# Hybrid RG-LRU and RWKV-7 block: two plain input-projection tiles go from the first stage to the preparation of the second recurrence

## The chip, the cores and the metric

The kernel runs on one core of a Trainium2 chip. The metric is device time in microseconds (us) of one execution. The engines are PE (TensorE matmul), PEld (TensorE weight load, which overlaps PE), DVE (VectorE), ACT (ScalarE), POOL (GpSimd) and SP (SyncE, which issues nearly all DMAs here).

## The reference, cut to what matters

One layer with 1024 latent tokens and 256 context tokens, model width 1024. The modulated input `h` is projected once by `w_in`; the columns of the product are split between the RG-LRU branch (`ux`, `uy`), the RWKV-7 branch (`r`, `k`, `v` and small low-rank inputs) and the two merge gates (`gl`, `gr`):

```python
ux_l, uy_l, zr_l, gl_l, gr_l = jnp.split(h_lat @ p['w_in'], pts, axis=-1)
hf_l, _ = lru_dir(ux_l, sf, p, 0, False)          # first recurrence, both directions
hb_l, _ = lru_dir(ux_l, sb, p, 1, True)
lru_l = ((hf_l + hb_l) * jax.nn.gelu(uy_l)).astype(h_lat.dtype)
rw_l, _ = rwkv_branch(centred_shift(to_colmajor(zr_l, rows), p['rwkv_mu']), S_c, p, True)
out_l = merge(lru_l, rw_l, gl_l, gr_l, p)         # sigmoid(gl), sigmoid(gr) as gates
```

After it follow the output projection, a SwiGLU channel mixer and a final norm. `uy`, `gl` and `gr` are used only after the second recurrence has begun, so their projection can be done at any time before that.

## The kernel before, in words

All projections run as float32 split in two parts: `mm3` (L87 to L90) issues three matmuls of 128x512 per 128x128 weight block, and so every output tile of 128 channels costs 8 blocks x 3 matmuls per 512 tokens. `inproj` (L218) computes one tile `m` of `w_in`: it loads the weights in two halves (`wraw`, 256 KB each), DVE casts each half to the high part (`whi`, L230), POOL subtracts for the low part (`wlo`, L231), and PE runs the matmuls into PSUM tiles named `pin{m}_{column}`. The tiles by number: 0 to 9 are `ux`, 10 to 19 `uy`, 20 to 27 `r`, 28 to 35 `k`, 36 to 43 `v`, 44 to 46 the low-rank inputs, 47 to 54 `gl`, 55 to 62 `gr`. (The small projection `w_gd2` in `gate` carries number 47 too.)

A *plain* tile is one of the 26 tiles of `uy`, `gl` and `gr`. `plain` (L289) is a generator that computes them one by one: 2 x 24 matmuls over the latent tokens, then ACT copies each PSUM half to `ev` (L296) and SP stores it to DRAM (L297). Nothing in the two stages below reads them.

**First stage**, `phase_ux` (L243): the ten `ux` tiles, then `NFILL - NEND` plain tiles with the eight `v` tiles spread evenly among them (for-loops at L266 to L277), then `NEND` = 3 plain tiles. The first recurrence (`lru_tiles`, 36 units of DVE, ACT, POOL and PE work) runs through all of this as a generator that is advanced at given points: after plain tile number q it has come to step 24 x (4 + 2 x min(1, (q+1)/10)). A `v` tile is projected over all 1280 tokens, shifted on DVE and ACT (`zv`, L493, L499), transposed on PE and stored.

**Preparation of the second recurrence**, `phase_a2` (L813): first the low-rank inputs (tiles 44 to 46, the first two over 1280 tokens) and the output gate, then ten units (0 and 1 for the context, 2 to 9 for one head pair each). A unit projects `k` and `r`, and in four sub-steps builds the operands of the second recurrence (`pz`, `kb`, `kr`, `kt`, `pm`, `km`). After units 1, 3, 5, 7, 8 and 9 their 32x32 triangular matrices are inverted on DVE (`wkv_inverse`, L724 and L725, 31 steps), in pieces between the sub-steps of the next units. The plain tiles that `phase_ux` left over are filled in by `due(x)`: after sub-step x of 40, x/38 of the `26 - NFILL` tiles must have been issued.

The second recurrence and everything behind it (`phase_b`, `phase_c1`, `phase_c2`) follow. The order of instructions on each engine is laid out when the program is built, by a scheduler that takes priorities from the code; on the chip each engine works through its own list in that order.

Of the kernel before, what the change touches and what calls it, by code (L numbers as in the profile page):

```python
# [242 lines left out]
def phase_ux(k):  # L243
    nc = k.nc
    k.inbufs = 3
    with k.tc.tile_pool(name="pux", bufs=1) as pool, k.tc.tile_pool(name="psux", bufs=2, space=PSUM) as ps, \
# [17 lines left out]
        fill = plain(k)  # L264
        n = NFILL - NEND
        for q in range(n):  # L266
# [13 lines left out]
            next(fill)  # L280


NFILL = 15
VEV = 2
INLO = 1
POFF = 400
# [526 lines left out]
def phase_a2(k, hc):  # L813
# [3 lines left out]
    with tc.tile_pool(name="pprep", bufs=1) as k.prep, tc.tile_pool(name="pzr", bufs=1) as k.zrp, tc.tile_pool(name="pa2c", bufs=1) as cp, \  # L817
# [50 lines left out]

        fill = plain(k, NFILL)
        nd = FILLA  # L870
# [3 lines left out]
        def due(x):  # L874
            for (a, b), (c, d) in zip(FPTS, FPTS[1:]):
                if x <= c:
                    return (b + (d - b) * (x - a) / (c - a)) * (26 - NFILL)
            return 26 - NFILL

# [806 lines left out]
```

## Time and profile before

| what | us |
|---|---|
| median of the runs (3 runs, 3083.84 to 3108.86) | 3095.47 |
| the profiled execution | 3079.55 |
| its span, first to last instruction | 3077.7 |
| PE busy, PEld busy | 2707.6 (88%), 2159.6 (70%) |
| DVE busy, ACT busy, POOL busy | 1890.6, 1456.4, 1012.4 (61%, 47%, 33%) |

The span falls into four parts: `ux` up to about 285 us, `v`, plain tiles and first recurrence up to about 715, the preparation of the second recurrence up to about 1520, and the rest. The changed lines lie in the second and third. A row of the windows view gives the busy time of each engine in a stretch, the count of instructions, the granted TensorE clock (1.00 is 2.4 GHz, 0.50 is 1.2 GHz) and the DMA share. Busy shares are averages; what a stretch is bounded by is read from the waits in it.

### The profile page before, as it was taken

Reading aid. Unit: us, or ns where it says so; the run is one execution under the profiler, and the core shown is the slowest. Engines: PE = TensorE matmul, PEld = TensorE weight load, DVE = VectorE, ACT = ScalarE, POOL = GpSimd, SP = SyncE. Lnnn points to the kernel's source line nnn. Section 1 sums busy time; section 2 is a strip of 40 time slices with the busy share of each in tenths; the row PEclk is TensorE's granted clock in tenths of the full one; section 3 lists DMA queues with packets and bytes.
Section 4 is the critical chain, followed back from the end, with each engine's and each line's share of the span. In section 5 each row is a group of like instructions: output and inputs, shape, how many; then the busy total and the mean of one; then the engine's idle time right before and its main releaser. Section 6 shows DMA issues by size and latency. Waiting matters only on the chain. (4 is left out here: it accounts for less than half of the span.)

```text
span 3077.7 us, 57133 instructions
## 1 busy us (share of the span) xinstructions
PE 2707.6 (88%) x22526; PEld 2159.6 (70%) x22526; DVE 1890.6 (61%) x2843; ACT 1456.4 (47%) x2647; POOL 1012.4 (33%) x896
## 2 busy tenths in 40 slices
PE   5988988889899878887889788777999999999998
PEld 4776766667677666676656666555788888888888
DVE  7588898994667977889872333564785323223234
ACT  3476777783467565767433343454334111111114
POOL 4344444452445555666333130235431000000000
PEclk9899999999999979988569998888999999999999
DMA  5333334322455456556766787988753111121112
GB/s 207 95 117 123 124 104 134 111 85 77 133 152 146 119 123 141 124 137 158 200 196 218 228 258 220 253 252 261 269 214 127 58 48 50 41 61 42 42 57 73
DMA packets 379602, 429.18 MB, mean 139 GB/s; under 512 B 134166, under 2 KB 286150, under 8 KB 371398
## 3 DMA queue, kind: packets, MB, share of 16 engines
q1 hardware_dynamic: 379334, 425.53, 47.4%
q8 instruction: 178, 2.92, 0.4%
q14 instruction: 90, 0.74, 0.1%
HBM read 286.87 MB, written 126.26 MB: 134 GB/s over the span
## 5 line engine op out<-in xcount | busy, mean ns | idle before, releaser
L88 PE MATMUL pin<-h1024hi,whi 128*128 128x512 f32 (+1 forms) x1024 | 430.5, 421 | 47.5 <-DVE whi L230 15.4
L90 PE MATMUL pin<-h1024hi,wlo 128*128 128x512 f32 (+1 forms) x1024 | 420.9, 414 | 10.7 <-POOL wlo L231 10.6
L89 PE MATMUL pin<-h1024lo,whi 128*128 128x512 f32 (+1 forms) x1024 | 425.8, 416 | 4.1 <-DVE h1024lo L120 4.1
L231 POOL TENSOR_TENSOR wlo<-wraw,whi 128x512 fp32r<-128x512 f32 (+1 forms) x144 | 211.7, 1471 | 306.6 <-DVE whi L230 167.8
L88 PEld LDWEIGHTS pin<-h1024hi,whi 128*128 128x128 f32 (+1 forms) x1024 | 203.3, 199 | 102.0 <-DVE whi L230 15.9
L90 PEld LDWEIGHTS pin<-h1024hi,wlo 128*128 128x128 f32 (+1 forms) x1024 | 201.5, 197 | 64.5 <-POOL wlo L231 17.7
L89 PEld LDWEIGHTS pin<-h1024lo,whi 128*128 128x128 f32 (+1 forms) x1024 | 203.4, 199 | 50.0 <-DVE h1024lo L120 6.6
L54 ACT ACT_TABLE_LOAD x164 | 210.4, 1283 | 18.3 <-DVE gd L499 5.9
L987 PE MATMUL pn<-tvu,ska 128*64 128x64 f32 (+1 forms) x2496 | 157.4, 250 | 36.1 <-ACT tvu L990 19.2
L1434 DVE TENSOR_TENSOR sil<-sil,pfu 128x512 f32<-128x512 f32 x44 | 30.3, 688 | 242.0 <-PE pfu L90 242.0
L388 DVE SCALAR_TENSOR_TENSOR lxc<-lup,c_lru_conv_w,lxc 120x512 f32<-120x512 f32 (+3 forms) x198 | 161.1, 837 | 15.9 <-ACT lxc L386 15.2
L987 PEld LDWEIGHTS pn<-tvu,ska 128*64 128x64 f32 (+1 forms) x2496 | 119.9, 156 | 71.8 <-ACT tvu L990 23.8
L1442 DVE SCALAR_TENSOR_TENSOR x<-pfo,modv,x 128x512 f32<-128x512 f32 (+1 forms) x112 | 74.2, 671 | 132.4 <-PE pfo L90 132.4
L990 ACT COPY tvu<-ru 32x256 f32<-32x256 f32 x193 | 70.1, 363 | 126.8 <-DVE tvu L990 77.8
L68 ACT CAST whi_fi<-wraw_fi 128x1024 fp32r<-128x1024 f32 x48 | 50.5, 1053 | 167.6 <-PE pfg L89 50.4
L724 DVE TENSOR_TENSOR it<-bp,X 128x62 f32<-128x62 f32 (+25 forms) x186 | 122.1, 657 | 3.9
L230 DVE CAST whi<-wraw 128x512 fp32r<-128x512 f32 (+1 forms) x144 | 76.3, 531 | 76.3 <-PE pin L89 36.6
L687 ACT COPY bc<-pm 32x256 f32<-32x256 f32 x160 | 98.8, 617 | 50.9 <-PE pm L683 48.4
L673 PE MATMUL pkt<-c_ident,kb 128*128 128x128 f32 x320 | 59.2, 315 | 65.6 <-DVE kb L657 41.5
L987 PE MATMUL ru<-tvu,skb 128*32 128x64 f32 (+1 forms) x2560 | 93.0, 243 | 26.8 <-ACT tvu L990 8.7
L725 DVE TENSOR_TENSOR X<-X,it 128x62 f32<-128x62 f32 (+25 forms) x186 | 113.7, 611 | 3.9
L432 POOL TENSOR_TENSOR lxc<-la 120x512 f32<-120x512 f32 (+3 forms) x66 | 86.8, 1318 | 80.1 <-ACT la L54 68.3
(374 smaller groups left out, 7512.9 us busy)
## 6 DMA issues: line engine op xcount, KB each, us to landing
skb<-skb_d SPq DMA_DIRECT2D x40, 1024.0 KB
wraw<-in_w_in_dram SPq DMA_DIRECT2D x142, 256.0 KB
wraw_fi<-in_w_ffn_in_dram SPq DMA_DIRECT2D x48, 512.0 KB
skb_d<-kr SPq DMA_DIRECT2D x160, 128.0 KB
ska_d<-kt SPq DMA_DIRECT2D x160, 128.0 KB
skb_d<-km SPq DMA_DIRECT2D x160, 128.0 KB
ska<-ska_d SPq DMA_DIRECT2D x40, 512.0 KB
wmr<-in_w_modT_dram SPq DMA_DIRECT2D x32, 512.0 KB
```

Source lines behind the costliest of these rows:

```text
L54: ins = self.nc.scalar.activation(*a, **b).ins
L88: nc.tensor.matmul(out, wh, xh, start=first, stop=False)
L89: nc.tensor.matmul(out, wh, xl, start=False, stop=False)
L90: nc.tensor.matmul(out, wl, xh, start=False, stop=last)
L230: nc.vector.tensor_copy(hi, raw)
L231: (nc.gpsimd if INLO else nc.vector).tensor_tensor(lo, raw, hi.bitcast(F32), ALU.subtract)
L388: nc.vector.scalar_tensor_tensor(xc, tap(j), k.lcw[r, t, d, j:j + 1], xc, ALU.mult, ALU.add)
L432: nc.gpsimd.tensor_tensor(xc, a, a, ALU.mult)
L687: nc.scalar.copy(bc[g, :, 4 * i:4 * i + 4].rearrange("s t e h -> s h e t"), pm[64 * c + 32:64 * c + 64, :, d, :, 32:64])
L724: nc.vector.tensor_tensor(tv, bpt[:, :, t + 1:32, t:t + 1].to_broadcast(sh), X[:, :, t:t + 1, 0:t + 1].to_broadcast(sh), ALU.mult)
L725: nc.vector.tensor_tensor(X[:, :, t + 1:32, 0:t + 1], X[:, :, t + 1:32, 0:t + 1], tv, ALU.add)
L987: k.pe_last = nc.tensor.matmul(*a, **b, start=True, stop=True).ins.name
```

## The change

```diff
-NFILL = 15
+NFILL = 13
```

`NFILL` stands in two places. In `phase_ux` the loop that carries the eight `v` tiles now runs over 10 plain tiles and not 12; the three at the end stay. In `phase_a2`, `plain(k, NFILL)` begins two tiles earlier in the list and `due` spreads 13 tiles and not 11 over the same 40 sub-steps. Every tile keeps its own work: the counts of instructions on PE, DVE, POOL and SP are the same, and ACT has 162 table loads for 164.

**End of the first stage, ACT.** Here the copies out of PSUM show in which order the tiles end: `ev49`, `ev50`, `ev51` are plain tiles, `vt7` is the last `v` tile, `held16` the first low-rank tile (`pin44`) of the next stage, `lg010_1_1` and `la10_1_1` belong to the last unit of the first recurrence. Before:

```order
L296 COPY ev49_0_5981<-pin49_0_5919 128x512
L572 COPY vt7_0_5892<-pv7_0_5893 128x512
L296 COPY ev49_512_5984<-pin49_512_5920 128x512
L572 COPY vt7_512_5900<-pv7_512_5901 128x512
L296 COPY ev50_0_6049<-pin50_0_5987 128x512
L572 COPY vt7_1024_5908<-pv7_1024_5909 128x256
L296 COPY ev50_512_6052<-pin50_512_5988 128x512
L296 COPY ev51_0_6117<-pin51_0_6055 128x512
L296 COPY ev51_512_6120<-pin51_512_6056 128x512
L509 COPY held16_6261<-pin44_0_6171 128x512
```

All of these stand behind the last step of the first recurrence. Now:

```order
L54 ACTIVATE lg110_1_1_5642<-pg10_1_1_5633,c_lru_bx_510 80x512
L296 COPY ev49_0_5981<-pin49_0_5919 128x512
L54 ACT_TABLE_LOAD
L54 ACTIVATE lg010_1_2_5425<-lg010_1_2_5425 80x512
L54 ACT_TABLE_LOAD
L54 ACTIVATE la10_1_1_5649<-lg010_1_1_5640,cneg_543 80x512
L54 ACTIVATE lg010_1_1_5640<-lg010_1_1_5640,cpos_540 80x512
L296 COPY ev49_512_5984<-pin49_512_5920 128x512
L54 ACT_TABLE_LOAD
L54 ACTIVATE lg010_1_1_5640<-lg010_1_1_5640 80x512
L509 COPY held16_6125<-pin44_0_6035 128x512
```

The last plain tile of the stage (49) now ends inside the last unit of the recurrence; tiles 50 and 51 are gone from here, the last `v` tile has moved ahead of the recurrence's end, and the first low-rank tile follows at once.

**The same place, DVE.** The operations of the last unit of the recurrence (`lg010_1_1`, `la10_1_1`, `lho10`) and the weight casts (`whi45` is the second low-rank tile). Now:

```order
L434 SCALAR_TENSOR_TENSOR lg010_1_1_5640<-lxc10_1_1_5409,lg010_1_1_5640 80x512
L445 TENSOR_TENSOR lg010_1_1_5640<-lg010_1_1_5640,lg110_1_1_5642 80x512
L447 SCALAR_TENSOR_TENSOR la10_1_1_5649<-la10_1_1_5649,la10_1_2_5432,lg010_1_1_5640 80x512
L455 TENSOR_TENSOR lho10_5647<-la10_0_1_4950,la10_1_1_5649 80x8x64
L230 CAST whi45_0_6154<-wraw45_0_6152 128x512
```

Before, five weight casts of the tiles 50, 51 and 44 stood between `lho10` and `whi45`; now `whi45` follows on `lho10` directly.

**Preparation, end of the third inverse, DVE.** `X4` is the matrix being inverted, `xo4` its result, `whi60` and `whi61` the weights of plain tiles, `zr8` the next `r` tile. Before:

```order
L734 STREAM_TRANSPOSE xo4_13265<-X4_11705 64x32x32
L658 SCALAR_TENSOR_TENSOR av5_256_1_12596<-kk7_12010,av5_256_1_12596 128x256
L657 TENSOR_TENSOR kb5_0_1_12633<-kd15_0_1_12630,ep5_0_1_12625 128x8x32
L689 TENSOR_TENSOR km4_768_1_12466<-pm4_768_12425,msk_6169 128x512
L230 CAST whi61_0_13282<-wraw61_0_13280 128x512
L230 CAST whi61_1_13312<-wraw61_1_13310 128x512
L499 SCALAR_TENSOR_TENSOR zr8_12771<-pin26_0_12772,c_mu_545,zr8_12771 128x512
```

Now:

```order
L725 TENSOR_TENSOR X4_11705<-X4_11705,it4_30_13262 128x2x31
L733 STREAM_TRANSPOSE xo4_13265<-X4_11705 64x32x32
L734 STREAM_TRANSPOSE xo4_13265<-X4_11705 64x32x32
L733 STREAM_TRANSPOSE xo4_13265<-X4_11705 64x32x32
L734 STREAM_TRANSPOSE xo4_13265<-X4_11705 64x32x32
L230 CAST whi60_1_12968<-wraw60_1_12966 128x512
L499 SCALAR_TENSOR_TENSOR zr8_12703<-pin26_0_12704,c_mu_545,zr8_12703 128x512
```

A whole plain tile (61) stood behind the third inverse; now half of tile 60 stands behind it and the other half inside it. Of the halves of plain tiles, 18 of 22 stood ahead of the third inverse's end before, and 21 of 26 stand there now. Counted over all projection tiles (plain, `k` and `r`), the inverse after unit 1 and the stretch behind it hold as many as before; the inverse after unit 3 holds half a tile more, the stretch behind it half a tile more, the inverse after unit 5 half a tile more, the stretch behind it as many, and the inverse after unit 7 half a tile more. That makes the two tiles.

## Rows read from the trace of the kernel before

**Rows 1.** Windows: busy us per engine (instructions), granted clock, DMA share; first stage.
```profile
285.00:690.00 405.00, 349.48 (x1540) 268.70 (x1539) 362.54 (x496) 307.94 (x460) 188.86 (x159) 0.95 0.36 111
690.00:710.00 20.00, 14.25 (x60) 11.24 (x59) 10.23 (x14) 16.56 (x22) 6.91 (x5) 0.83 0.12 34
710.00:790.00 80.00, 78.90 (x370) 60.51 (x369) 40.05 (x70) 19.93 (x30) 20.02 (x21) 1.00 0.26 80
```
**Rows 2.** Waits of DVE and of PE, 285 to 690: total us, times, longest.
```profile
DVE lg L445 <- ACT lg L54: 23.4, 6, 6.0
DVE lg L434 <- POOL lxc L432: 7.1, 8, 1.6
...
PE pg L415 <- DVE ll L399: 11.0, 9, 3.2
```
**Rows 3.** Timeline of PE: start us, us, engine, line; spacing of projection matmuls.
```profile
714.87 0.40 PE L88 MATMUL pin<-h1024hi,whi 128*128 128x512 f32 x1
...
717.20 0.40 PE L89 MATMUL pin<-h1024lo,whi 128*128 128x512 f32 x1
...
698.48 0.63 PE L89 MATMUL pin<-h1024lo,whi 128*128 128x512 f32 x1
...
701.47 0.63 PE L90 MATMUL pin<-h1024hi,wlo 128*128 128x512 f32 x1
...
317.99 0.28 PE L88 MATMUL pin<-h256hi,whi 128*128 128x256 f32 x1
...
318.70 0.28 PE L88 MATMUL pin<-h256hi,whi 128*128 128x256 f32 x1
```
**Rows 4.** Timeline: last gate matmul, last recurrence step, start of the second low-rank tile.
```profile
686.68 0.39 PE L415 MATMUL pg<-lh,gw 80*80 80x512 f32 x1
...
712.06 1.04 DVE L455 TENSOR_TENSOR lho<-la,la 80x512 f32<-80x512 f32 x1
...
751.28 0.40 PE L88 MATMUL pin<-h1024hi,whi 128*128 128x512 f32 x1
```
**Rows 5.** Operations on the tile zv (a v tile), DVE: duration ns min/median/max.
```profile
L499 DVE SCALAR_TENSOR_TENSOR zv<-held,c_mu,zv x32: 723/742/1796, 340.2 to 709.5; 128x512 f32<-128x512 f32 x16, 128x511 f32<-128x511 f32 x16
...
L499 DVE SCALAR_TENSOR_TENSOR zv<-pin,c_mu,zv x16: 452/472/486, 342.6 to 710.2; 128x255 f32<-128x255 f32 x16
```
**Rows 6.** Windows: preparation of the second recurrence, inverses and stretches between them.
```profile
790.00:979.00 189.00, 175.61 (x1401) 145.46 (x1399) 118.46 (x186) 126.65 (x272) 100.35 (x114) 0.95 0.61 159
979.00:1061.00 82.00, 67.15 (x523) 51.74 (x524) 79.72 (x120) 45.71 (x89) 46.28 (x47) 0.88 0.49 119
1061.00:1116.00 55.00, 36.54 (x371) 29.91 (x371) 35.66 (x56) 41.68 (x85) 33.17 (x41) 0.74 0.61 134
1116.00:1190.00 74.00, 59.41 (x423) 46.79 (x422) 72.56 (x107) 33.88 (x66) 35.00 (x35) 0.87 0.46 108
1190.00:1272.00 82.00, 77.21 (x659) 62.79 (x660) 53.70 (x83) 55.83 (x111) 55.62 (x63) 0.96 0.59 140
1272.00:1350.00 78.00, 62.84 (x515) 50.63 (x513) 76.09 (x114) 46.83 (x91) 44.20 (x46) 0.89 0.51 123
1350.00:1407.00 57.00, 55.38 (x504) 45.52 (x505) 43.80 (x65) 42.82 (x86) 39.35 (x45) 0.94 0.64 158
1407.00:1486.00 79.00, 47.77 (x554) 39.17 (x552) 77.25 (x116) 54.95 (x101) 51.58 (x58) 0.70 0.74 189
```
**Rows 7.** Weight casts (L230) and weight subtractions (L231), 790 to 1486: ns min/median/max.
```profile
L230 DVE CAST whi<-wraw x68: 363/428/1554, 791.3 to 1410.3; 128x512 fp32r<-128x512 f32 x68
...
L231 POOL TENSOR_TENSOR wlo<-wraw,whi x69: 1263/1307/1742, 788.8 to 1410.8; 128x512 fp32r<-128x512 f32 x69
```
**Rows 8.** Timeline of DVE and POOL: inverse steps beside a weight subtraction.
```profile
995.31 0.61 DVE L725 TENSOR_TENSOR X<-X,it 128x440 f32<-128x440 f32 x1
...
998.37 1.71 DVE L724 TENSOR_TENSOR it<-bp,X 128x462 f32<-128x462 f32 x1
...
998.13 1.45 POOL L231 TENSOR_TENSOR wlo<-wraw,whi 128x512 fp32r<-128x512 f32 x1
```
**Rows 9.** Windows: end of the preparation and start of the second recurrence.
```profile
1440.00:1450.00 10.00, 3.95 (x44) 3.55 (x44) 9.75 (x19) 5.89 (x6) 7.45 (x8) 0.50 0.78 193
...
1500.00:1540.00 40.00, 38.39 (x397) 26.96 (x397) 33.08 (x83) 11.95 (x23) 9.35 (x13) 0.50 0.62 154
1540.00:1580.00 40.00, 34.46 (x357) 23.10 (x357) 31.56 (x50) 16.72 (x29) 13.13 (x11) 0.51 0.69 193
```

## The prediction

> **What bounds the kernel now.** The page gives shares over the whole span, and these hide that the two stages the change touches have different limits. So I read the windows view first, stage by stage, and in each stretch looked for the engine that is never free.
>
> In the stretch with `v`, plain tiles and the first recurrence, 285 to 690 us, no engine is full: DVE is busy 362.5 of 405 us (90%), PE 349.5 (86%), ACT 307.9 [rows 1]. What DVE waits for there is the recurrence itself: ACT for `lg` 23.4 us, POOL for `lxc` 7.1 us, and PE in turn waits for DVE to make `ll` [rows 2]. So the stretch is paced by a chain that goes round DVE, ACT and POOL, and PE's projection tiles lie in its holes, not always neatly. From 710 to 790 the picture turns: PE is busy 78.9 of 80 us at full clock, DVE half [rows 1]. There the recurrence is over, and PE works off what is left of the stage: plain tiles, then the low-rank tiles that open the next stage.
>
> The preparation alternates. While an inverse runs (979 to 1061, 1116 to 1190, 1272 to 1350, 1407 to 1486), DVE is busy 97 to 98% and PE 60 to 82%; between them PE is the fuller one (77.2 of 82 us, 55.4 of 57 us) and DVE has room [rows 6]. A plain tile in an inverse can be nearly free; one in the stretch between costs its own length.
>
> **The price of a tile.** At full clock, eleven projection matmuls of 512 columns begin between 714.87 and 717.20, so one takes 0.233 us; at half clock eight begin between 698.48 and 701.47, 0.427 us each; those of 256 columns follow at 0.118 us, 317.99 to 318.70 being six steps [rows 3]. A plain tile is 48 of the first: 11.2 us of PE, or 20.5 at half clock. A `v` tile has 24 short ones besides: 11.2 + 2.8 = 14.0 us. On the other engines a plain tile has two casts on DVE of 0.43 us and two subtractions on POOL of 1.31 us [rows 7]. Its DMAs, two loads of 256 KB and two stores of the same size, go with it; in the stretches where it arrives the DMA share is 0.46 to 0.74 [rows 6], so I cost them at nothing, with 0.74 in the last inverse as the weakest cover. If that cover is gone, the moved traffic of a tile (1 MB, at the 0.19 MB per us of that stretch) would take some 5 us.
>
> **Part 1, the end of the first stage.** Before, the last gate matmul of the recurrence begins at 686.68 and the second low-rank tile at 751.28: 64.6 us [rows 4]. Between them PE has the rest of the last `v` tile (by the order, nearly half), three plain tiles (33.6) and the first low-rank tile (14.0), and stretches in which it is idle or at a lower clock (5.8 us idle and 0.83 of the clock from 690 to 710 [rows 1]). Now the order holds there only the rest of one plain tile, 4 us, and the first low-rank tile, 14.0: 18 us of PE. But one wait takes the place of that work: the second low-rank tile's cast `whi45` stands on DVE behind the last step of the recurrence, `lho`. That step began 25.4 us after the last gate matmul and took 1.0 [rows 4]; with the cast it makes 27 us. Behind `whi45` waits PE with all the low-rank tiles, and behind these the whole next stage. So the 64.6 us become 18 at the least (chain of the recurrence out of the way sooner, since the `v` tile's six DVE operations no longer stand in it: 4 x 0.742 + 2 x 0.472 = 3.9 us [rows 5]) and 27 at the most. I take 24: **41 us less**, bounds 37 to 46.
>
> **Part 2, the recurrence's own stretch.** Not all of that is gain. The `v` tile that stood behind the recurrence now lies inside it. By count of matmuls in the order, PE has 13.7 us more to do from the last `ux` tile to the last gate matmul, and DVE 3.9 + 0.8 us. If all of PE's addition lands on the chain, the stretch grows by 14; if it falls into the 55 us of PE's idle time there [rows 1], by nothing. PE stands still there mostly because it waits for the chain, but in its own fixed order, so holes are used only in part. Nearer the upper end, since PE is 86% full: **11 us more**.
>
> The first stage thus ends about 30 us sooner (bounds 23 to 46), more than the 22.4 us of the two tiles, because the `v` tile is drawn into the holes as well.
>
> **Part 3, the preparation.** By the order, the additional two tiles come out as half a tile each in the inverses after units 3, 5 and 7, and half a tile in the stretch between 1190 and 1272. The last half: 5.6 us of PE where PE is at 94% [rows 6], so 5.6 us on the path. The other three halves, 16.8 us of PE, lie in inverses in which PE is idle for 14.6, 15.2 and 31.2 us [rows 6]; what is left on the path is what they take from DVE: three casts, 1.3 us, and what POOL's three subtractions do to the inverse. One can be seen in the timeline [rows 8]: a step of 462 elements takes 1.71 us while a weight subtraction runs beside it, where one of 440 elements took 0.61. That is 1.0 us for each, 3 us in all. Part 3 costs 5.6 + 1.3 + 3 = **10 us**. The bounds: 1 us, the casts alone, if PE and POOL find holes everywhere; and 27 us if both tiles lie whole on the path, 22.4 + 4.4.
>
> The Trainium skill, page "SBUF — State Buffer", section "SBUF: two separate sides", says that VectorE operations with two SBUF inputs and GpSimd operations share one pair of ports as an exclusive lock, and that the loser stands for the whole instruction. By that rule it would be 1.31 us for each subtraction in an inverse, 3.9 and not 3 us; the trace agrees in kind (1.71 for about 0.65).
>
> **The sum.** -41 + 11 + 10 = -20 us. Against the profiled execution that is 3079.55 - 20 = 3059.6. That execution was itself 15.9 us under the median of the runs shown; against the median, 3095.5 - 20 = **3075.5**. What a measurement of this kernel can tell from no change is about 1%, 31 us, and this is under it.
>
> **The rivals.**
>
> *PE's total is all that counts.* PE is 86% busy in the first stage and not far from it in the preparation, so both could be bounded by its total: the first stage gives back just 22.4 us and the preparation takes just 22.4. For it: the stretches between the inverses, 55.4 of 57 us. Against it: four inverses of 74 to 82 us with PE at 60 to 82%. Time 3095.5.
>
> *The preparation loses more than the first stage gives.* The mechanism: PE works through its list in order, and a half tile inside an inverse stands in front of the transposes and `pm` matmuls whose results DVE's own list needs between two inverse steps; DVE then stands too, and at a low clock a tile costs 20.5 and not 11.2 us. The place is the last two inverses, where the clock was 0.89 and 0.70 over the stretch [rows 6]. The price is two tiles at half clock, 41 us, against a gain of 23 to 30 in the first stage: +11 to +18, 3106 to 3114. It decides from the point where DVE in the inverses shows over 10 us of waiting for PE; before, it is idle only 1.4 to 2.3 us in each.
>
> *The clock at the end.* PE falls to 3.95 busy of 10 us at 1440 to 1450, the granted clock falls to 0.50 with it, and it stays at 0.50 and 0.51 up to 1580 though PE is busy 72.9 of 80 us from 1500 on [rows 9]. The last plain tile now lies half a tile later, just ahead of that hole. If that keeps PE busy through it and the clock stays up, half of these 72.9 us is the most that can come back, 36; I take 18: a sum of -38, 3057.5. Against it: the inverse after unit 7 goes on for another 40 us with PE at about half, and the hole is far longer than half a tile. The Trainium skill, page "TensorE: Matmul & The Clock Gate", section "What's actually happening", has the throttled clock as the default, which activity releases; it fits these rows and does not say on which side of it half a tile would land.
>
> *It does nothing at all* is no rival of its own here: the two tiles are seen to move in the order, and only their cost is in question; that is the first rival.
>
> **How the numbers follow.** Chances: the forecast 0.58 (own range -40 to 0, from 37 to 46 less, 0 to 14 more and 1 to 27 more, whose ends are not taken together), PE's total 0.17, preparation loses more 0.10, clock 0.15. In the runs shown, single times lie 12 us under and 13 us over the median, so each case is spread by about 10 us. The forecast and the clock case reach down to 3050; leaving out the upper rival's far end, the range reaches up to 3106. Faster by over 1% (below 3064.5): nearly all of the clock case and an eighth of the forecast, 0.20. Slower by over 1% (above 3126.4): the upper rival with a spread in its direction and what I have not thought of, 0.06. The rest, 0.74, lies within 1%.
>
> **What would show it.** In the first stage: the second low-rank tile begins about 24 us after the last gate matmul of the recurrence, not 65, and that gate matmul comes at 687 plus at most 14. If it comes later than 701, part 2 is wrong and the recurrence is held up by PE after all. In the preparation: from the first low-rank tile to the last inverse it should grow by about 10 us; the four inverses should stay within 2 us of 82, 74, 78 and 79, and only the stretch behind the second should grow. Inverses that grow by more than 5 us with DVE idle in them mean the second rival; DVE full and steps at 1.0 us and more beside POOL mean the port. The stages from the second recurrence on should keep their length, apart from the clock at its start.

## The result, and the profile after

The change makes the kernel slower by 0.6%. The median is 3103.60 us (3092.06 to 3112.20, 20 runs) against 3083.85 us of before beside it (3073.88 to 3108.86, 20 runs); the ratio is 1.0058, with a 95% interval of 1.0046 to 1.0070, so 18 us. That lies inside the range of the prediction, within 1%, and on the other side of zero from the 20 us that it named. The range held by luck: it was counted from 3095.47, the median of three runs, and counted from 3083.85 the same sum gives 3064 and a range that ends at about 3094.

The profiled execution has a span of 3094.8 us against 3077.7: 17.1 us to find. The timelines give the places. After, with the rows that answer to [rows 4] first, then the first low-rank cast (`lora`), the first step of the second recurrence (`ru`), the last transposition of the last inverse (`xo`) and the first output matmul (`py`):

```profile
702.29 0.40 PE L415 MATMUL pg<-lh,gw 80*80 80x512 f32 x1
...
724.38 1.06 DVE L455 TENSOR_TENSOR lho<-la,la 80x512 f32<-80x512 f32 x1
...
727.61 0.40 PE L88 MATMUL pin<-h1024hi,whi 128*128 128x512 f32 x1
...
740.64 2.05 DVE L808 CAST lora<-lz 64x1024 fp32r<-64x1024 f32 x4 [0.87 <-ACT lz L54]
...
1480.18 1.08 PE L987 MATMUL ru<-tvu,skb 64*32 64x64 f32 x32 [0.51 <-DMA skb<-skb_d]
...
1604.68 1.99 DVE L734 STREAM_TRANSPOSE xo<-X 64x1024 f32<-64x1024 f32 x1
...
1688.58 0.24 PE L987 MATMUL py<-tvu,skb 128*32 128x64 f32 x1
```

The last four in the kernel before:

```profile
758.39 1.73 DVE L808 CAST lora<-lz 64x1024 fp32r<-64x1024 f32 x3 [2.07 <-ACT lz L54]
...
1461.62 0.85 PE L987 MATMUL ru<-tvu,skb 64*32 64x64 f32 x22
...
1607.11 1.95 DVE L734 STREAM_TRANSPOSE xo<-X 64x1024 f32<-64x1024 f32 x1
...
1677.75 0.24 PE L987 MATMUL py<-tvu,skb 128*32 128x64 f32 x1
```

So the low-rank cast comes 17.8 us sooner. The last inverse ends at 1606.7 and not 1609.1: only 2.4 us of these are left, the preparation has taken 15.4. And the first output matmul follows 81.9 us behind that end and not 68.7: 13.2 more, which makes it 10.8 us late. What is left of the 17.1 us, 6, comes after it; from the first output matmul to the end of the span before took 1400 us, after 1406, and most of the kernels below between 1394 and 1411 (e7, which has the order of before from the low-rank cast on, 1417), so 6 us there says little.

The windows show what the engines did. From 285 us to the last gate matmul, before and after, and under them ACT's wait for the gate matmuls (285 to 687, 285 to 702):

```profile
285.00:686.68 401.68, 346.17 (x1526) 266.28 (x1524) 361.43 (x494) 304.65 (x456) 186.80 (x157) 0.95 0.36 112
285.00:702.29 417.29, 357.89 (x1604) 277.37 (x1605) 369.61 (x503) 309.42 (x468) 199.42 (x160) 0.96 0.37 111
...
ACT lg L54 <- PE pg L415: 11.6, 7, 3.7
...
ACT lg L54 <- PE pg L415: 18.0, 9, 5.1
```

The stretch is 15.6 us longer. PE is busy for 11.7 us more in it and idle for 59.4 us and not 55.5, although a `v` tile was to fall into its holes there. ACT, a link of the recurrence's chain, waits 6.4 us longer for PE's gate matmuls.

After, from 710 to 790, and what DVE does there once the recurrence's last step (724.38) and one weight cast are done:

```profile
710.00:790.00 80.00, 67.45 (x315) 50.88 (x316) 55.36 (x82) 30.86 (x48) 21.64 (x23) 0.91 0.21 65
...
731.46 0.17 DVE L534 TENSOR_SCALAR ka<-c_rwkv_k_a 128x8 f32<-128x8 f32 x1 [5.76 <-DMA c_rwkv_k_a<-in_rwkv_k_a_dram]
```

PE is no longer full (67.45 of 80, before 78.90). DVE waits 5.76 us for a small constant of the next stage, whose operation stands ahead of the first low-rank tile's in DVE's list. Before, it waited 6.7 us for the same constant, but this was over at 720, 31 us ahead of the second low-rank tile, while PE still worked on plain tiles.

The same view for the later stretches. After: first low-rank cast to the last step of the last inverse but one; the stretch of the last inverses by the clock; the last inverse's end to the first output matmul:

```profile
740.60:1542.30 801.70, 668.07 (x5582) 533.90 (x5580) 639.89 (x984) 477.28 (x958) 432.43 (x477) 0.87 0.57 139
1440.00:1600.00 160.00, 108.06 (x1210) 78.50 (x1208) 140.33 (x231) 80.59 (x157) 80.74 (x86) 0.57 0.74 193
1606.70:1688.60 81.90, 75.83 (x1010) 53.18 (x1010) 21.11 (x39) 25.45 (x53) 28.79 (x18) 0.98 0.78 235
```

Before, the same three:

```profile
758.40:1541.00 782.60, 665.63 (x5643) 531.97 (x5643) 627.45 (x983) 480.22 (x959) 429.92 (x473) 0.86 0.57 141
1440.00:1600.00 160.00, 124.30 (x1470) 89.72 (x1470) 136.41 (x240) 74.92 (x144) 69.13 (x73) 0.58 0.76 208
1609.10:1677.80 68.70, 64.98 (x698) 44.70 (x699) 15.28 (x28) 20.31 (x40) 26.05 (x17) 0.89 0.73 226
```

Two things are to be seen. The preparation is 19.1 us longer up to here, but PE did only 2.4 us more in it, although 73 projection matmuls more lie in it (17 us; two tiles have 96, but 23 others now come ahead of the cast): something else was pushed out, and the count in the last stretch shows what. Between the last inverse's end and the first output matmul PE has 1010 matmuls to do after and 698 before. Some 112 of them in either kernel belong to the output projection of the RG-LRU branch (`pol`); the rest are of the first eight steps of the second recurrence (the context), which run beside the last inverses as far as they get. What is left over comes behind, where PE is busy 93% and 95%. From 1440 to 1600 PE was busy 16.2 us less. What it waited for there, after, and under it the two longest waits of before:

```profile
PE pkt L673 <- DVE kb L657: 17.9, 5, 6.6
PE pm L683 <- DVE km L689: 12.8, 5, 6.6
PE pn L987 <- issue: 8.1, 1, 8.1
PE pkt L673 <- DVE bonus L697: 4.2, 1, 4.2
...
PE pkt L673 <- DVE kb L657: 23.0, 6, 6.2
PE pkt L673 <- POOL kb L659: 4.4, 1, 4.4
```

In both kernels PE stands in front of the matmuls of the last units (`pkt`), whose operands DVE makes between steps of the inverses, and before for longer. New are 12.8 us in front of `pm`, which waits for DVE to empty the `pm` tile before (`km`), and 8.1 us for nothing that the profile shows. The recurrence's steps stand behind in PE's list.

Where the preparation grew shows when it is cut at the inverses. After: up to the first inverse, then in turn an inverse (its first step to its last transposition) and the stretch behind it, as in [rows 6], up to the end of the fourth; under them the time of the steps of the four inverses (operations on the tile `it`), before and after:

```profile
740.64:965.96 225.32, 202.82 (x1475) 161.23 (x1474) 144.57 (x229) 132.57 (x281) 105.70 (x116) 0.95 0.53 137
965.96:1043.89 77.93, 63.57 (x521) 51.01 (x519) 76.56 (x114) 45.26 (x87) 44.31 (x45) 0.90 0.49 117
1043.89:1105.31 61.42, 43.14 (x484) 36.49 (x488) 43.37 (x62) 45.78 (x93) 41.07 (x51) 0.78 0.64 141
1105.31:1173.53 68.22, 57.14 (x356) 44.98 (x349) 66.26 (x98) 25.57 (x48) 25.26 (x24) 0.93 0.43 105
1173.53:1259.99 86.46, 82.45 (x722) 66.89 (x722) 55.77 (x88) 61.58 (x124) 62.23 (x70) 0.97 0.65 154
1259.99:1347.50 87.51, 72.11 (x576) 57.23 (x575) 85.31 (x123) 50.03 (x98) 46.25 (x47) 0.86 0.48 113
1347.50:1411.11 63.61, 55.26 (x459) 44.11 (x460) 48.91 (x67) 42.72 (x85) 42.92 (x49) 0.89 0.61 147
1411.11:1486.30 75.19, 50.31 (x510) 41.11 (x509) 73.27 (x109) 49.36 (x91) 44.12 (x49) 0.73 0.56 141
...
sum 313.38, DVE 175.66; mean DVE 43.92
...
sum 308.85, DVE 178.32; mean DVE 44.58
```

By the same bounds the eight were 220.7, 82.7, 54.3, 73.7, 82.4, 78.1, 56.9 and 78.9 us before. So three of the four inverses are shorter by 3.7 to 5.4 us, the third is 9.4 us longer, and together they take 4.5 us less. All four stretches ahead of an inverse are longer: by 4.7, 7.2, 4.1 and 6.7 us, together 22.7. Of these PE is busy for 8.0 us and idle for 14.6.

### The profile page after: what moved, and what is told of

It reads as the page before. It is cut to its first block, busy times and chain, and to the rows that moved or that the text cites. A ratio compares the mean times of both kernels' runs of the same rounds, so it can differ in the third digit from the quotient of the medians.

```text
span 3094.8 us, 57092 instructions
## 1 busy us (share of the span) xinstructions
PE 2693.0 (87%) x22526; PEld 2148.7 (69%) x22526; DVE 1915.4 (62%) x2843; ACT 1451.4 (47%) x2645; POOL 1019.1 (33%) x896
## 5 line engine op out<-in xcount | busy, mean ns | idle before, releaser
L88 PE MATMUL pin<-h1024hi,whi 128*128 128x512 f32 (+1 forms) x1024 | 429.0, 419 | 53.7 <-DVE whi L230 15.4
L231 POOL TENSOR_TENSOR wlo<-wraw,whi 128x512 fp32r<-128x512 f32 (+1 forms) x144 | 216.8, 1506 | 301.4 <-DVE whi L230 157.8
L987 PE MATMUL pn<-tvu,ska 128*64 128x64 f32 (+1 forms) x2496 | 147.7, 244 | 40.9 <-ACT tvu L990 22.5
L987 PEld LDWEIGHTS pn<-tvu,ska 128*64 128x64 f32 (+1 forms) x2496 | 113.4, 151 | 70.9 <-ACT tvu L990 25.9
L725 DVE TENSOR_TENSOR X<-X,it 128x62 f32<-128x62 f32 (+25 forms) x186 | 123.5, 664 | 4.1
L987 PE MATMUL ru<-tvu,skb 128*32 128x64 f32 (+1 forms) x2560 | 105.1, 242 | 22.1 <-DVE tvu L1048 9.0
L430 POOL TENSOR_TENSOR lg<-lg,lxc 120x512 f32<-120x512 f32 (+3 forms) x66 | 89.8, 1367 | 80.4 <-ACT lg L54 80.1
L69 POOL TENSOR_TENSOR oll<-olr,olh 128x640 fp32r<-128x640 f32 x32 | 53.6, 1695 | 189.2 <-ACT olh L68 127.2
L230 DVE CAST whi<-wraw 128x512 fp32r<-128x512 f32 (+1 forms) x144 | 79.3, 553 | 56.7 <-DMA wraw<-in_w_in_dram 32.7
```

The source lines that it names most:

```text
L88: nc.tensor.matmul(out, wh, xh, start=first, stop=False)
L230: nc.vector.tensor_copy(hi, raw)
L231: (nc.gpsimd if INLO else nc.vector).tensor_tensor(lo, raw, hi.bitcast(F32), ALU.subtract)
L430: nc.gpsimd.tensor_tensor(gi, gi, xc, ALU.mult)
L725: nc.vector.tensor_tensor(X[:, :, t + 1:32, 0:t + 1], X[:, :, t + 1:32, 0:t + 1], tv, ALU.add)
L987: k.pe_last = nc.tensor.matmul(*a, **b, start=True, stop=True).ins.name
```

## The experiments

In all of them the table gives: the first low-rank cast, the first `ru`, the end of the last inverse, the preparation (cast to that end), the hand-over (that end to the first `py`), and the ratio to the kernel before with its interval. The times are those of one profiled execution each, the ratio is of the kernels' runs. "15" and "13" are the plain tiles in the first stage.

| kernel | cast | first ru | end | prep. | hand-over | ratio |
|---|---|---|---|---|---|---|
| before (15) | 758.4 | 1461.6 | 1609.1 | 850.7 | 68.7 | |
| after (13) | 740.6 | 1480.2 | 1606.7 | 866.1 | 81.9 | 1.0058 [1.0046, 1.0070] |
| e1 | 737.0 | 1475.9 | 1601.8 | 864.8 | 88.7 | 1.0040 [1.0022, 1.0059] |
| e2 (13) | 739.6 | 1460.9 | 1617.5 | 877.9 | 87.6 | 1.0084 [1.0054, 1.0114] |
| e3 (15) | 759.0 | 1467.1 | 1636.1 | 877.1 | 76.8 | 1.0087 [1.0064, 1.0110] |
| e4 | 782.4 | 1476.0 | 1641.4 | 859.0 | 69.2 | 1.0078 [1.0050, 1.0106] |
| e5 | 758.8 | 1493.0 | 1629.9 | 871.1 | 85.4 | 1.0168 [1.0145, 1.0190] |
| e6 | 780.4 | 1486.1 | 1629.8 | 849.4 | 87.2 | 1.0105 [1.0090, 1.0119] |
| e7 | 762.9 | 1462.8 | 1610.8 | 847.9 | 67.6 | 1.0014 [0.9998, 1.0030] |
| e8 | 739.4 | 1477.0 | 1602.5 | 863.1 | 89.6 | 1.0032 [1.0013, 1.0050] |
| e9 (15) | 760.9 | 1453.2 | 1605.6 | 844.7 | 72.8 | 1.0015 [1.0001, 1.0028] |
| e10 (13) | 740.9 | 1442.5 | 1604.8 | 863.9 | 74.6 | 1.0000 [0.9987, 1.0014] |
| e11 (15) | 759.1 | 1460.6 | 1617.2 | 858.1 | 80.1 | 1.0065 [1.0047, 1.0083] |
| e12 (13) | 740.3 | 1469.3 | 1607.6 | 867.3 | 95.1 | 1.0081 [1.0061, 1.0100] |
| e13 | 741.4 | 1489.7 | 1609.3 | 867.9 | 80.4 | 1.0058 [1.0037, 1.0079] |
| e14 | 741.6 | 1459.9 | 1623.3 | 881.7 | 90.4 | 1.0110 [1.0086, 1.0134] |
| e15 | 757.5 | 1465.0 | 1604.6 | 847.1 | 70.8 | 0.9987 [0.9971, 1.0002] |
| e16 | 740.3 | 1438.6 | 1604.8 | 864.5 | 81.8 | 0.9986 [0.9969, 1.0003] |
| e17 (13) | 741.5 | 1437.6 | 1593.6 | 852.1 | 103.1 | 1.0043 [1.0019, 1.0068] |
| e18 (15) | 758.7 | 1434.0 | 1595.0 | 836.3 | 82.6 | 1.0050 [1.0031, 1.0069] |

**The first stage: the two tiles without the `v` tile, and the `v` tile without the two tiles.**

```diff
-NFILL = 15
+NFILL = 13
-NEND = 3
+NEND = 1
```

> Takes the two plain tiles away from the end of the first stage (NEND 1, NFILL 13), so that the loop with the v tiles has 12 plain tiles as in the kernel before, and the preparation is ordered as in the changed kernel. It tells what drawing the v tile into the recurrence's stretch did apart from the rest. If the v tile in the stretch is a gain (the prediction's view): the first low-rank cast comes later than the 740.6 us of the changed kernel, near 748, and the time is 6 to 8 us over the changed kernel's, about 3110. If PE's total alone counts: 740 and the same time, 3103. If the v tile stretches the recurrence by more than it frees behind it: last gate matmul at 687 as before, first low-rank cast at 758.4 - 22.4 = 736, and some 5 us under the changed kernel, 3098. In all three the preparation loses about 20 us against the kernel before, since its order is that of the changed kernel.

```diff
-NEND = 3
+NEND = 5
```

> 15 plain tiles in the first stage as before, but the eight v tiles are spread over ten of them and five stand at the end: the last v tile is drawn into the recurrence, and no plain tile changes stage. By the prediction's parts 1 and 2 that alone gains 7.6 us (41 less in the tail, 11 more in the recurrence, two plain tiles of 22.4 back in the tail): 3075. By the reading of the changed kernel against the kernel with two tiles taken from the end it costs about 5 us: 3088, with the last gate matmul at about 701.

e1 brings the cast forward by 21.4 us, nearly the 22.4 of two tiles; e8 and e16 below, whose first stage has the same code, by 19.0 and 18.1. By the ratios e1 is some 5 us faster than the changed kernel, but the two intervals overlap. In e7, whose order from the low-rank cast on is that of before, the last gate matmul comes at 705.0 and not 686.7, the cast 4.5 us later, and the whole at 1.0014: drawing the `v` tile in costs between nothing and 9 us, and a gain of 7.6 is outside the interval. It also shows how far two executions of one order differ: the preparation is 847.9 against 850.7, the hand-over 67.6 against 68.7. e1, in turn, has the order of the changed kernel from the cast on, and there the hand-over is 88.7 and 81.9, with the granted clock at 0.85 and 0.98.

**The price of two tiles at either place**, by doing two plain tiles twice: in the preparation (e5), at the end of the first stage (e6).

```diff
+    if start:
+        jobs += jobs[-REP:]            # e5: REP = 2, and due spreads 26 + REP - NFILL
     for m, dst, i in jobs[start:]:
```

> The first stage as before (15 plain tiles); the preparation does 13 plain tiles, the eleven of before and the last two of the list a second time. It measures what two more tiles cost where the change puts them, with nothing taken from the first stage. By the prediction's part 3 they cost 10 us: about 3093 against a before of 3083. By PE's length alone 22.4 us: 3105. By the reading of the changed kernel (19 us in the preparation itself, and about 13 more at the start of the second recurrence) some 32 us: 3115, with the first low-rank cast at 758, the last two inverses' ends some 19 us later than before, and the first output matmul of the second recurrence (py) at about 1709.

```diff
         for q in range(NEND):
             next(fill)
+        again = plain(k, NFILL - REP)
+        for q in range(REP):
+            next(again)
```

> The last two plain tiles of the first stage are done twice, behind everything else of it; the preparation keeps its eleven. It measures what a tile is worth at the place from which the change takes it. If PE is full there, as the windows say, two tiles are 22.4 us and this gives 3105, the first low-rank cast at 781, and all stages behind it keep their length. If the tail has room after all: under 15 us, 3098 and less. If the later stages don't depend on when they begin: no change at the end although the cast is later.

They cost 52 us (1.0168) and 32 us (1.0105). The difference, 19 us, is near the change's loss of 18, but this may be luck, since both are far above 22.4. In e6 the stage itself does as expected: the cast 22.0 us later, the last inverse's end 20.7. Then the hand-over is 18.5 us longer, though nothing was added there and the preparation has before's work; its order was laid out anew, with different places for DVE's operations beside the inverses. e5: 20.4 us in the preparation, 16.7 in the hand-over, and 23.5 more behind the first output matmul, in an execution that was itself 5 us over its kernel's median.

**The same change at other due points**: pairs of 15 and 13 tiles, in which the preparation's tiles are due after 33, 36 or 40 of the sub-steps instead of 38.

```diff
-FPTS = ((0, 0), (38, 1), (40, 1))
+FPTS = ((0, 0), (33, 1), (40, 1))     # e2 (NFILL = 13), e3 (15)
+FPTS = ((0, 0), (36, 1), (40, 1))     # e10 (13), e9 (15)
+FPTS = ((0, 0), (40, 1))              # e12 (13), e11 (15)
```

> The changed kernel (NFILL 13) with the 13 plain tiles of the preparation due by sub-step 33 of 40, not 38. Theory A, the buffers of the second recurrence are free only when the last projection tile is done: its first load of skb came 12 us after the last store of a plain tile's result before (1439.9 to 1451.6) and 26 us after it in the changed kernel (1446.4 to 1472.4); with the last plain tile some 50 us sooner the last r tile becomes the gate, the first load comes by 1455, and the second recurrence reaches its first py matmul at 1678 or sooner, about 10 us or more better than the changed kernel: 3085 to 3095. Theory B, the preparation ends with the DVE inverses and the recurrence starts when they let it: tiles moved forward only lengthen what is in front, the first load keeps its distance to the last inverse, and the time stays at 3100 to 3110.

> The kernel before (NFILL 15) with its 11 plain tiles due by sub-step 33 of 40. Theory A: the last tile was the gate here too (last store 1440.9, first load 1448), so this gains a little, 5 to 10 us: 3074 to 3079. Theory B: no gain, 3084 or a few us more, since tiles that lay in the last inverse, where PE was idle for 31 of 79 us, now lie in fuller stretches.

> The plain tiles of the preparation are due after 36 of the 40 sub-steps instead of 38, 15 in the first stage: the same work in the same stages as before, with the tiles a little sooner, so that the scheduler lays out a slightly different order. If the time follows from the work of each stage (two tiles more in the preparation cost what they cost), this is the kernel before: 3079 to 3088. If the order before is an especially good one for the passage into the second recurrence, and most others are worse, this is 10 to 27 us slower: 3094 to 3111, with the first output matmul (py) about 90 us behind the last inverse's end and not 72.

> The change in question, two tiles from the first stage to the preparation, with the tiles due after 36 sub-steps. If two tiles cost more in the preparation than at the end of the first stage by their work, this is about 18 us slower than the run with 15 tiles due by 36. If the loss is that of one good order, the two differ by no more than 8 us, on either side. The prediction's own prices would make it 20 us faster.

> The plain tiles of the preparation are due after all 40 sub-steps, 15 in the first stage: the tiles a little later than before. By the stages' work: as before, 3079 to 3088. By the good order: 3094 to 3111.

> The change in question with the tiles due after 40 sub-steps. By the stages' work some 18 us slower than the run with 15 tiles due by 40; by the good order within 8 us of it; by the prediction's prices 20 us faster than it.

From the ratios, 13 tiles against 15 make -1 us (33), -5 (36), +18 (38, the change) and +5 (40). In all four the cast comes 18 to 20 us sooner. The preparation grows by 1, 19, 15 and 9 us, the hand-over by 11, 2, 13 and 15. So the change as such is worth +4 us in the mean of four that lie up to 23 us apart. Preparation and hand-over together grow by 12, 21, 29 and 24 us, in the mean 21, which is about the 22.4 us of PE that the two tiles need; and in all four pairs the stretches ahead of the first four inverses grow (13, 24, 23, 28 us) while these inverses together become shorter (by 13, 13, 5, 12). An early start alone doesn't decide: in e2 the first load of the second recurrence came at 1454.0 and in the changed kernel at 1472.4, and e2 is no faster. With 15 tiles alone, where only the due point differs and the work is the same, the kernels lie between 1.0000 and 1.0087: where the tiles lie and the order that comes of it are worth 27 us, more than the two tiles' move. e9 does not speak for one lucky order: its order differs from before, and at 5 us slower it lies where the other theory, the stages' work, had it (3079 to 3088), and not 10 us and more behind.

The windows of the hand-over, e10 (with the preparation up to the last inverse but one ahead of it), e1 and e3:

```profile
740.90:1540.40 799.50, 684.11 (x5796) 541.54 (x5797) 633.28 (x990) 479.30 (x962) 429.17 (x477) 0.87 0.57 141
...
1604.80:1679.40 74.60, 68.11 (x755) 48.17 (x756) 15.93 (x29) 21.30 (x42) 27.50 (x17) 0.94 0.70 212
```

```profile
1601.80:1690.50 88.70, 84.23 (x1008) 58.40 (x1008) 21.09 (x39) 25.41 (x53) 28.71 (x18) 0.85 0.69 217
```

```profile
1636.10:1712.80 76.70, 69.16 (x721) 47.72 (x720) 16.26 (x30) 21.64 (x43) 28.71 (x18) 0.84 0.70 217
```

e10 and the changed kernel have the same tiles, and preparations of 864 and 866 us. But e10 starts its recurrence 38 us sooner, PE gets 684.1 us of work done up to the last inverse but one and not 668.1, and 755 matmuls are left over and not 1010. Its hand-over is 7.3 us shorter, and its first output 9.2 us sooner; the other half of the 18.5 us between the two spans comes behind that, and these rows don't explain it. e1 and the changed kernel have the same count left (1008, 1010) and differ in the clock, 0.85 and 0.98; e3 and before (721, 698) in the clock too, 0.84 and 0.89. Nor does the count alone set the hand-over: e9 has 950 matmuls left and takes 72.8 us, e5 has 714 and takes 85.4, at clocks of 0.92 and 0.80.

**Two tiles fewer in the preparation.**

```diff
-NFILL = 15
+NFILL = 17
```

> The change in the other direction: NFILL 17, two more plain tiles in the first stage and 9 in the preparation. If the change lost by what it put into the preparation (a tile there costs more than it frees in the first stage), this is faster than before by about as much, 3066 to 3075. If the first stage and the preparation are balanced at 15 (a minimum), this is slower too, 3090 to 3100: the first stage 22 us longer, the preparation 10 us shorter. If PE's total counts: 3084.

The cast is 24.0 us later, and the preparation, with two tiles less, is not shorter but 8.3 us longer (859.0); the ratio makes 24 us in all. The change and its mirror image both lose, and a preparation that grows by losing two tiles is not explained by the tiles' work.

**What holds the second recurrence back.** In the changed kernel the first load of `skb` is issued at 1472.44, before at 1451.64. Four kernels to move this: the last plain tile one sub-step sooner in e1 (e8), two sub-steps sooner in the changed kernel (e14), two later in before (e15), and the loads alone raised in priority in the changed kernel (e13).

```diff
-                while nd < due(4 * u + i + 1):
+                while nd < due(4 * u + i + 1) or (4 * u + i + 1 == 35 and nd < 26 - NFILL):   # e8; e14: 34
+                while nd < due(4 * u + i + 1) and (nd < 25 - NFILL or 4 * u + i + 1 >= 37):   # e15
-SETO = 0
+SETO = 3000                                                                                   # e13
```

> As the kernel with two tiles taken from the end (which took 12 us more than before), but the last plain tile of the preparation is issued one sub-step sooner, as in the kernel before; every other tile stays. If the start of the second recurrence waits for that tile's result store, and this is what makes the second recurrence late, the first skb load comes at about 1452 instead of 1467, the first output matmul (py) some 12 us sooner, and the whole 3084. If the start doesn't set the second recurrence's length (PE's total from 1440 to 1690 does), the load may come sooner, and the time stays at 3095.

> The changed kernel, but its last plain tile is issued two sub-steps sooner (34 of 40 instead of 36), directly behind the one before it; all the others stay. If the last tile's place holds the second recurrence back, the first skb load comes at 1435 to 1455 instead of 1472, and the time falls to 3080 to 3090. If not, it stays within 5 us of 3104.

> The kernel before, but its last plain tile is issued two sub-steps later (37 of 40 instead of 35). If the last tile's place holds the second recurrence back, the first skb load comes later than 1452, at 1465 to 1475, the first output matmul 10 to 15 us later than 1678, and the time is 3092 to 3102. If not, it stays within 5 us of 3083.

> The changed kernel (13 plain tiles in the first stage, due after 38 sub-steps), with the first loads of the second recurrence raised in priority: up to them the lists of SP, POOL and DVE stay as they are, then they stand ahead of the km, kt and kr stores in SP's list. If the late start is what the changed kernel loses, the first skb load comes some 10 us sooner than 1472, the first output matmul 5 to 10 us sooner than 1689, and the whole at 3088 to 3096 instead of 3104. If the order beside the inverses is the cause, or the tile's own store and POOL's memset hold the loads whatever stands ahead of them, it stays within 4 us of 3104.

The theory that the last tile's place is the cause finds no support. In e8 the load did not move (1467.3, as in e1), and DVE, ACT and POOL have e1's order from the cast on, so it tells nothing of this; it is a second execution of that order, with a hand-over of 89.6 us and 88.7. In e15 the load came 5 us later (13 and more were expected), and the kernel lost nothing. In e13 the load came 16 us sooner, at 1456.2, and the first step 10 us later, at 1489.7; the ratio is that of the change, 1.0058. PE's timeline in e13 shows why:

```profile
1460.75 1.13 PE L683 MATMUL pm<-kr,kb 64*64 64x64 f32 x32 [3.73 <-DVE km L689]
...
1471.19 1.13 PE L683 MATMUL pm<-kr,kb 64*64 64x64 f32 x32 [6.55 <-DVE km L689]
...
1488.64 1.13 PE L683 MATMUL pm<-kr,kb 64*64 64x64 f32 x32 [7.09 <-DVE km L689]
1489.71 1.08 PE L987 MATMUL ru<-tvu,skb 64*32 64x64 f32 x32
```

The data are there, but the step stands behind three `pm` groups, each of which waits for DVE to empty the tile before (`km`), 17.4 us together. And e14 shows the other side: the load at 1452.9 and the first step at 1459.9, as hoped, and the kernel is still 16 us slower than the changed one (1.0110 against 1.0058). The last units are late: from 1480 to 1610 DVE's listed waits come to 23.9 us, the longest for PE's `pbn` (6.3) and ACT's copies, and to 14.9 in the changed kernel. The last inverse ends 16.6 us later than in the changed kernel. So an early start is neither enough nor always good. That steps of the recurrence and operands of the last units compete for places in PE's and ACT's lists is the likely reason, and is not shown apart from the rest of the order.

**The two best parts together** (13 tiles, one at the end, due by 36).

```diff
-NFILL = 15
+NFILL = 13
-FPTS = ((0, 0), (38, 1), (40, 1))
-NEND = 3
+FPTS = ((0, 0), (36, 1), (40, 1))
+NEND = 1
```

> 13 plain tiles in the first stage, taken from its end so that the v tiles stay spread over twelve, and due after 36 sub-steps. Without the drawn-in v tile the changed kernel was some 5 us faster, and with 36 sub-steps some 24 us faster than as it is: together 3075, 5 us faster than the kernel before. If the two don't add, 3080 to 3085.

0.9986, and e15 0.9987: both intervals take in 1. No kernel here beats the one before by more than its measurement can tell. e16 has e10's order from the cast on; its hand-over is 81.8 us and not 74.6, at a clock of 0.81 and not 0.94.

**POOL's part in the preparation's price**: in the pair due by 36, the low weights of the preparation's plain tiles come from ACT, which copies the raw weights into their place; the subtraction is left out, so `uy`, `gl` and `gr` of these tiles are not those of the reference.

```diff
-            (nc.gpsimd if INLO else nc.vector).tensor_tensor(lo, raw, hi.bitcast(F32), ALU.subtract)
+            if act:                            # only for the plain tiles of the preparation
+                nc.scalar.copy(lo, raw)
+            else:
+                (nc.gpsimd if INLO else nc.vector).tensor_tensor(lo, raw, hi.bitcast(F32), ALU.subtract)
```

> The changed kernel with tiles due by 36 (3079.7), but the low part of the weights of the preparation's 13 plain tiles is not subtracted on POOL: ACT copies the raw weights into its place, so uy, gl and gr of these tiles are not the reference's. 26 operations of 1.3 us leave POOL. If POOL's subtractions are what lengthens DVE's operations in the preparation, at about 1 us each, the stretch from the first low-rank cast to the last inverse's end falls from 859.9 by 15 to 25 us, and the inverse's two operations (L724, L725) from 643 and 635 ns to under 625 each. If PE's length or the order is what counts, it stays within 8 us of 860.

> The same at 15 tiles in the first stage: 22 operations leave POOL. If the subtractions are the price, the stretch falls from 840.9 by 12 to 22 us, and the gap of 19 us between 13 and 15 tiles shrinks to under 12. If PE's length is the price, the gap stays between 15 and 22.4 us.

The groups by line: of e17 the copies on ACT and the inverse's two operations, of e18 the same two operations.

```profile
L232 ACT CAST wlo<-wraw 128x512 fp32r<-128x512 f32 x26 | 16.0, 614 | 11.9 <-DMA wraw<-in_w_in_dram 6.6 <-PE pin L90 5.3
L727 DVE TENSOR_TENSOR it<-bp,X 128x62 f32<-128x62 f32 (+25 forms) x186 | 115.1, 619 | 4.1
L728 DVE TENSOR_TENSOR X<-X,it 128x62 f32<-128x62 f32 (+25 forms) x186 | 117.7, 633 | 4.2
...
L727 DVE TENSOR_TENSOR it<-bp,X 128x62 f32<-128x62 f32 (+25 forms) x186 | 121.1, 651 | 3.9
L728 DVE TENSOR_TENSOR X<-X,it 128x62 f32<-128x62 f32 (+25 forms) x186 | 121.4, 653 | 3.9
```

The preparation is 11.8 us shorter at 13 tiles (26 operations) and 8.4 at 15 (22), less than the 15 to 25 and 12 to 22 that POOL as the cause was to give. (The 859.9 and 840.9 of the expectations end at the last inverse's last step, 4 us ahead of the table's end.) The gap between 13 and 15 is 15.8 us, and was 19.2; under 12 was expected of POOL, 15 to 22.4 of PE's length. And the inverse's operations did not fall as expected: in e17 to 619 and 633 ns from 643 and 635, and in e18 they rose, to 651 and 653 from 635 and 640 in e9. Both orders were laid out anew, so this pair gives no price for a subtraction, and does not show POOL to be what the preparation costs. And once more the hand-over takes more than the preparation gave: 103.1 us at 13, with 1010 matmuls left at a clock of 0.82,

```profile
1593.60:1696.60 103.00, 94.92 (x1010) 64.98 (x1010) 20.55 (x38) 25.63 (x53) 28.66 (x18) 0.82 0.60 181
```

so that a last inverse that ends 11 us sooner gives a first output 17 us later.

## Why the prediction was wrong, point by point

**Part 1 was right for what it counted.** The second low-rank tile begins 25.3 us behind the last gate matmul (702.29 to 727.61), 24 were said, and before it was 64.6 [rows 4]: 39.3 us less, bounds 37 to 46. What it left out is the way from there to the `lora` cast: 13.0 us after, and 7.1 before. DVE's wait for the constant (5.76 us, until 731.46) stands in it now; before it was over while PE still worked off the plain tiles. PE waits with it (67.45 of 80 us busy, [rows 1] 78.90).

**Part 2 is the first step that failed.** It took 11 us, with 14 as the upper bound, and so made the drawn-in `v` tile a gain. The last gate matmul came 15.6 us later, in e7 18.3; the prediction's own sign, later than 701, is there. The step that failed is "holes are used only in part": none was used. PE's idle time up to the last gate matmul is 59.4 us and was 55.5, so the tile's work came on top, and the chain waited longer for PE's gate matmuls (18.0 us, before 11.6). Parts 1 and 2 together were to give 30 us, and gave 17.8 at the cast; leaving the `v` tile out gave 18.1 to 21.4 (e16, e8, e1).

**Part 3 was mis-sized, within its bounds, and had the place wrong.** 10 us were said (1 to 27). It was 15.4 here, and 1, 19, 9 at the other due points: 11 in the mean. The step that failed is that three of the four half tiles, lying in inverses in which PE is idle, cost no more than their casts and POOL's part. The inverses, which were to stay within 2 us, moved by -5 to +9 and take 4.5 us less together; the stretches ahead of them, of which only the one behind the second was to grow, all grew, by 22.7 us. The inverses hold about a dozen DVE operations fewer than before and the stretches about a dozen more, so units' work that was done beside the inverses now stands between them; what pushed it there is not shown. The term for POOL, 3 us for three subtractions, is not contradicted: the steps of the four inverses take 178.32 us and took 175.66, 2.7 more (-2 to +5 at the other due points). The Trainium skill's page "SBUF — State Buffer", section "SBUF: two separate sides", has the loser of the shared ports stand for the whole instruction; by it the prediction's estimate was 3.9 us. The 2.7 us measured lie nearer to the 3, and no run here isolates the lock.

**The term that was missing is the hand-over.** The prediction closed with "The stages from the second recurrence on should keep their length, apart from the clock at its start". They did not: 13.2 us came there, and over the four pairs 2 to 15. The sum by stages leaves out that stages overlap: eight steps of the second recurrence run in the preparation's gaps on PE, and here fewer of them got done there. With what was measured the sum is -39 (part 1) +16 (part 2) +6 (to the cast) +15 (preparation) +13 (hand-over) +6 (behind it) = +17 us (the span: 17.1), where -41 + 11 + 10 = -20 was said. How much of the 13 is the count of matmuls left and how much the clock is open: e1 and e8, with the same order and count, have 88.7 and 89.6 us at 0.85 and 0.87, the changed kernel 81.9 at 0.98.

**The rivals.** "PE's total is all that counts" comes nearest for the four due points together: preparation and hand-over take 21 us in the mean for the tiles' 22.4, the cast gives 18 to 20, and the move is worth +4 us. For this change alone it says 0, and 18 came. "The preparation loses more" had the sign, and its 11 to 18 us, but by luck, for its mechanism is not there: in the third and fourth inverse DVE is idle 2.2 and 1.9 us, where over 10 of waiting for PE were to decide. "The clock at the end" did not happen: from 1440 to 1600 the clock is 0.57, and was 0.58.

**What stays open.** Why the scheduler's order at 38 sub-steps and 13 tiles passes on 1010 matmuls and at 36 only 755 is seen in PE's list (the steps stand behind `pm` groups that wait for `km`), but no single place was found that cures it: raising the loads (e13) and moving the last tile (e8, e14) did not. How much of the preparation's growth is the tiles' own work and how much their order was not taken apart either; it is 1 us at one due point and 19 at another. Why PE is idle 14.6 us longer in the stretches between the inverses was not traced.

## What to carry to other kernels

Before a sum by stages, look for the next stage's work that already runs in this stage's gaps: filler that is added there can take the gaps from that work, and the price then shows up one stage later. And where a scheduler lays out the lists anew at every change, time the change at two or three neighbouring settings of a number that leaves the work as it is: here the setting alone was worth 27 us, and one pair would have given 18 us for a move that is worth -5 to +18, in the mean about 4.

## What the runs showed that was not expected

The same order repeats to 3 us in the preparation (e7 and before; e1, e8 and the changed kernel; e16 and e10), but not behind it. The hand-over of one order lies up to 8 us apart (81.9, 88.7, 89.6), and from the first output matmul to the end e7 took 1417 us and before 1400. So differences of 10 us in the preparation are more than executions of one order show; in the hand-over, and still more behind the first output matmul, one execution of each is too little for them. The granted clock of the hand-over differs between executions of one order without an evident reason, 0.85 in e1 and 0.98 in the changed kernel, with 1008 and 1010 matmuls: 84.2 and 75.8 us of PE.
